# Block sums of the normed tokens formed by TensorE in PSUM, with the x rows loaded first, in a decoder layer on one core

## The chip, the core and the metric

The program runs on one core of a Trainium2 chip. TensorE (PE) multiplies matrices and writes to PSUM, eight banks of 128 partitions x 512 f32 words; VectorE (DVE), ScalarE (ACT) and GpSimd (POOL) work on elements; SyncE (SP), ACT and POOL issue DMA transfers between the chip's memory and the core's SBUF. Each engine works through its own instructions in order and waits on semaphores of the others. The metric is the device time of one execution in microseconds (us), lower is better. All times here are of this one core.

## What is computed

One decoder layer on 512 tokens of width 1024: a SwiGLU feed-forward block (FFN 1), a mixer (RWKV-7 heads beside differential attention), and a second feed-forward block (FFN 2), each with an RMS norm before and after:

```python
for l in range(DEPTH):
    h = rmsnorm(x, ffn1_pre_g[l])
    x = x + FFN_RES * rmsnorm(swiglu(h, ffn1_w_gate[l], ffn1_w_up[l], ffn1_w_down[l]), ffn1_post_g[l])
    h = rmsnorm(x, mix_pre_g[l])
    ...
    x = x + rmsnorm(y, mix_post_g[l])
    h = rmsnorm(x, ffn2_pre_g[l])
    x = x + FFN_RES * rmsnorm(swiglu(h, ffn2_w_gate[l], ffn2_w_up[l], ffn2_w_down[l]), ffn2_post_g[l])
```

with `rmsnorm(x, g) = x * rsqrt(mean(x * x) + eps) * g` per token and `swiglu(h) = (silu(h @ w_gate) * (h @ w_up)) @ w_down`.

## The kernel before

**Precision.** The large products run on rounded operands (F32R). To keep f32 accuracy each operand is split into a rounded part and a remainder (`parts`: ACT rounds, DVE subtracts), and a product is three matmuls: high by high, high by low, low by high (L615, L617, L618 in the FFN).

**Strassen-Winograd blocks.** The gate and up products of an FFN (class `FFN`) take the 1024 input features in two halves and the 512 tokens in two halves. Seven products replace eight, numbered 1 to 7, for each of 11 pairs of weight tiles. Their token operands are `B11` and `B21` (the first 256 tokens, lower and upper features), `B22` (last 256 tokens, upper features) and four block sums, T1 = B12 - B11, T2 = B22 - T1, T3 = B22 - B12, T4 = B21 - T2. Each operand is stored as features on partitions, tokens along the row, split in two parts. The weight operands are sums as well (`g_weights`, on DVE) and are split by `wparts`.

**Slots.** `g_slots` lists 77 (pair, product) slots; a slot (`g_product`) is 24 matmuls of 128x128 by 256 columns. The first four need only B11 and B21; the fifth, (0, 5), needs T1. `stream` prepares the weights of a slot AHEAD = 2 slots before its products; they sit in three rotating pairs of tiles.

**Where the token operands come from.** `start` (FFN 1) loads the four token tiles of 128 rows, takes the norm's factor (`rms`, ACT squares and DVE reciprocal) and scales on ACT (L511). For FFN 2 `norms` does the same behind the output projection (tail key "o") and scales on DVE (L311). Then `feat` handles the tile: eight transposes of 128x128 f32 into two PSUM banks that take turns (L527), a multiplication by the gain on DVE from PSUM to an f32 buffer (`h32`, L530), and for tiles 0 and 1 the split into B11 and B21 (L494 on ACT, L495 on DVE). For tiles 2 and 3 DVE also forms T1, T2, T3 and T4 from `h32` (L538), and T1, T2, B22, T3 and T4 are split.

**What sets the order.** `Streams` interleaves generators by due times written into the code, and a scheduler then places the instructions of each engine; the resulting order is fixed in the program. The DMA queue of SP takes x tiles, weights and results in program order; the ACT queue takes the rows of gains.

Of the kernel before, what the change touches and what calls it, by code (L numbers as in the profile page):

```python
# [19 lines left out]
P = 128  # L20
T = 512
# [36 lines left out]
def layout(inputs):  # L58
# [38 lines left out]
    rows += [g["mix_pre_g"]]  # L97
# [4 lines left out]
    for p in range(NPR):  # L102
# [21 lines left out]
        "gnb": (3584, 512), "lam": (4096, 256), "gm": (4352, 1024)}  # L124


class Layer:
# [4 lines left out]
    def setup(self, st):  # L132
# [11 lines left out]
        nc.scalar.dma_start(out=self.ident, in_=A["ident"])  # L144
        self.zero = c.tile([P, 1], F32, name="zero")
# [132 lines left out]
    def norms(self, S, br, t, key, ys, half, xsrc, dst, h=None, tb=None, feat=None):  # L278
# [8 lines left out]
        xo, tmp, z = br["xo"][t], br["tmp"], br["z"][t % 2]  # L287
# [22 lines left out]
        if feat is not None:  # L310
            nc.vector.tensor_scalar(out=z, in0=xo, scalar1=r, scalar2=None, op0=ALU.mult)  # L311
            yield 0.0, 0.8
            yield from feat(t, z, tb)
            S.mark(f"{key}z{t}")
            S.mark(f"{key}h{t}", 1.2)
            return
# [57 lines left out]
    def run(self):  # L374
        tc, nc, A = self.tc, self.nc, self.A
        S = self.S = Streams()
        with ExitStack() as st:
# [34 lines left out]
            br = self.bridge(f2.big("F1"), fp, "pgm")  # L412
# [32 lines left out]
class FFN:  # L445
# [37 lines left out]
    def inputs(self):  # L483
        self.B = {n: self.hslot(n) for n in ("B11", "T1", "T2", "B21", "T3", "B22", "T4")}
        self.h32 = self.big("F2")[:, 0:4096].rearrange("p (b k t) -> p b k t", b=4, k=4)
        self.cb = self.bridge_tile()
        self.gst = ExitStack()
        self.gp = self.gst.enter_context(self.tc.tile_pool(name=f"gp{self.i}", bufs=1, reuse_waits="tile"))
        self.raw = {}
# [8 lines left out]
    def start(self, t, src):  # L498

        L, nc, S = self.L, self.nc, self.S  # L500
        if t == 0:
            self.x0 = self.big("F1")
        x = self.x0[:, t * D:(t + 1) * D]
        junk = self.x0[:, 4 * D:5 * D]
        nc.sync.dma_start(out=x, in_=src[t * P:(t + 1) * P, :])
        if t == 1:
            self.load(0, 0)
        yield 0.0, 2.0
        r = L.rms(x, junk, "p")
        yield 0.0, 2.5  # L510
        nc.scalar.activation(x, x, AF.Copy, scale=r)  # L511
# [4 lines left out]
    def feat(self, t, xn, tb):  # L516
# [4 lines left out]
        o, _ = FV[f"g{self.i}"]  # L521
        dst = lambda n: [self.B[n][:, i, :, cs] for i in range(2)]
        for q in range(2):
            pt = L.bank(tb, "pt")
            for j in range(4):
                k = q * 4 + j
                nc.tensor.transpose(pt[:, j * P:(j + 1) * P], xn[:, k * P:(k + 1) * P], L.ident)  # L527
            hv = self.h32[:, q * 2 + half, :, cs]
            g = L.fv[:, o + q * 4:o + q * 4 + 4].unsqueeze(2).to_broadcast([P, 4, P])
            nc.vector.tensor_tensor(out=hv, in0=pt.rearrange("p (k t) -> p k t", k=4), in1=g, op=ALU.mult)  # L530
            if half == 0:
                self.parts(hv, dst(("B11", "B21")[q]))
            yield 0.42, 0.3 if q == 0 else 0.0
        if half == 0:
            return
        B11, B12, B21, B22 = (self.h32[:, i, :, cs] for i in range(4))
        t1, t2, t3, t4 = (self.cb[:, i:i + 512].rearrange("p (k t) -> p k t", k=4) for i in (1024, 1536, 3072, 3584))
        sub = lambda o, a, b: nc.vector.tensor_tensor(out=o, in0=a, in1=b, op=ALU.subtract)  # L538
        sub(t1, B12, B11)
        self.parts(t1, dst("T1"))  # L540
        sub(t2, B22, t1)
        self.parts(t2, dst("T2"))
        self.parts(B22, dst("B22"))
        sub(t3, B22, B12)
        self.parts(t3, dst("T3"))
        sub(t4, B21, t2)
        self.parts(t4, dst("T4"))
        S.mark(f"{self.i}T{t}", 2.0)
# [100 lines left out]
    def stream(self):  # L649
# [8 lines left out]
        for i in range(self.AHEAD):  # L658
# [3 lines left out]
        for i, (m, p) in enumerate(slots):  # L662
# [4 lines left out]
            ahead(i + self.AHEAD)  # L667
            self.g_product(m, p, ws.pop(i))
            self.g_out(m, p)
            yield 2.87, 0.0  # L670
# [724 lines left out]
```

## Time and profile before

| | us |
|---|---|
| median of 3 runs | 1110.42 |
| lowest and highest of these runs | 1110.08, 1114.44 |
| the profiled execution | 1110.48 |
| its span, first to last instruction | 1108.7 |
| PE busy in the span | 1052.6 |
| DVE busy | 726.0 |
| ACT busy | 525.8 |
| POOL busy | 54.5 |

The profile shows one execution. Busy time of an engine counts its operations; the granted clock is TensorE's, as a share of full speed (1.00 is 2.4 GHz, 0.50 is 1.2 GHz). Matmuls are pipelined: a record of 0.28 us can be followed by the next after 0.12 us. A row of a group of instructions gives line, engine, operation, result and sources, shapes and count. FFN 1's products run from 20 to about 253 us, the mixer and the output projection to 737, FFN 2 from there to the end. A few matmul records can be missing from a trace.

### The profile page before, as it was taken

The numbers are of one execution on the slowest core, as the hardware profiler recorded it, in microseconds if no ns is written. First come the engines' busy times: TensorE is split into PE (matmuls) and PEld (weight loads), VectorE is DVE, ScalarE is ACT, GpSimd is POOL, SyncE is SP. The second block draws the span as 40 slices with busy tenths as digits, with TensorE's granted clock in tenths as the row PEclk, the third lists the DMA queues.
The fourth block names the chain that finished last, engine by engine and source line by source line (L and its number), as shares of the span: only waits on it lengthen the run. The fifth ranks groups of instructions, "written<-read, shape, count | busy, mean of one in ns | idle before, by whom it ended". The sixth has DMA issues, their size and how long they took to land.

```text
span 1108.7 us, 17430 instructions
## 1 busy us (share of the span) xinstructions
PE 1052.6 (95%) x7104; PEld 923.1 (83%) x7104; DVE 726.0 (65%) x1131; ACT 525.8 (47%) x849; POOL 54.5 (5%) x64
## 2 busy tenths in 40 slices
PE   4799999999999899999999999986999999999997
PEld 4799999998888696777778776776999999988886
DVE  5987888874333453577744797479888888753335
ACT  7555444553222766623453535365554554542223
POOL 0000000000000101222211110000000000000000
PEclk9899999999999899988998999988999999999999
DMA  7133333205333937653773426321424233043332
GB/s 306 40 114 127 103 92 137 77 1 171 95 95 95 247 94 163 144 118 86 174 175 92 91 57 233 101 95 42 149 79 143 85 114 116 1 152 95 95 95 96
DMA packets 52881, 127.11 MB, mean 115 GB/s; under 512 B 21688, under 2 KB 22072, under 8 KB 52800
## 3 DMA queue, kind: packets, MB, share of 16 engines
q1 hardware_dynamic: 45872, 106.18, 29.1%
q0 software_dynamic: 4320, 14.98, 8.2%
q10 hardware_dynamic: 2608, 4.83, 1.3%
q8 instruction: 56, 0.92, 0.3%
q14 instruction: 25, 0.20, 0.1%
HBM read 116.56 MB, written 7.34 MB: 112 GB/s over the span
## 4 chain that ended last, share of the span: by engine, by line
PE 87%; DVE 6%; ACT 3%; DMA 2%; issue 1%; ACTq 0%; POOL 0%; SPq 0%; DVEq 0%; POOLq 0%
PE gu L615 13%; PE gu L617 13%; PE gu L618 13%; PE y L220 8%; PE y L221 8%; PE y L222 8%; PE pj L220 4%; PE pj L221 4%; PE pj L222 4%; PE sc L1327 1%; PE op L1355 1%; DVE br L538 1%; PE s L1055 1%; DMA F<-in_x 1%; DMA raw<-in_gup 1%
## 5 line engine op out<-in xcount | busy, mean ns | idle before, releaser
L615 PE MATMUL gu<-T,w 128*128 128x256 f32 x704 | 199.9, 284 | 8.5 <-ACT T L494 8.5
L617 PE MATMUL gu<-T,w 128*128 128x256 f32 x704 | 200.0, 284 | 0.6 <-DVE T L495 0.6
L618 PE MATMUL gu<-T,w 128*128 128x256 f32 x704 | 198.6, 282 | 0.0
L494 ACT ACTIVATE w<-raw 128x1024 fp32r<-128x1024 f32 x110 | 116.7, 1061 | 127.2 <-issue 76.0
L209 DVE TENSOR_TENSOR wlo<-raw,whi 128x1024 fp32r<-128x1024 f32 x52 | 63.6, 1224 | 150.7 <-ACT whi L208 150.6
L615 PE MATMUL gu<-B,w 128*128 128x256 f32 x528 | 151.7, 287 | 9.4 <-ACT w L494 7.5
L617 PE MATMUL gu<-B,w 128*128 128x256 f32 x528 | 151.1, 286 | 0.9 <-DVE B L495 0.9
L495 DVE TENSOR_TENSOR w<-raw,w 128x1024 fp32r<-128x1024 f32 x110 | 134.5, 1223 | 24.5 <-ACT w L494 24.4
L618 PE MATMUL gu<-B,w 128*128 128x256 f32 x528 | 150.2, 285 | 0.0
L615 PEld LDWEIGHTS gu<-T,w 128*128 128x128 f32 x704 | 133.1, 189 | 8.7 <-ACT T L494 8.7
L220 PE MATMUL y<-whi,a 128*128 128x512 f32 x352 | 138.9, 395 | 0.0
L222 PE MATMUL y<-whi,a 128*128 128x512 f32 x352 | 138.9, 395 | 0.0
L221 PE MATMUL y<-wlo,a 128*128 128x512 f32 x352 | 138.9, 395 | 0.0
L618 PEld LDWEIGHTS gu<-T,w 128*128 128x128 f32 x704 | 134.5, 191 | 0.2 <-DVE w L495 0.2
L617 PEld LDWEIGHTS gu<-T,w 128*128 128x128 f32 x704 | 133.0, 189 | 0.9 <-DVE T L495 0.9
L208 ACT ACTIVATE whi<-raw 128x1024 fp32r<-128x1024 f32 x52 | 55.0, 1059 | 163.3 <-PE y L221 156.9
L615 PEld LDWEIGHTS gu<-B,w 128*128 128x128 f32 x528 | 101.4, 192 | 9.8 <-ACT w L494 7.7
L617 PEld LDWEIGHTS gu<-B,w 128*128 128x128 f32 x528 | 101.4, 192 | 1.2 <-DVE B L495 1.2
L618 PEld LDWEIGHTS gu<-B,w 128*128 128x128 f32 x528 | 101.9, 193 | 0.0
L220 PE MATMUL pj<-hm,whi 128*128 128x512 f32 x184 | 79.9, 434 | 0.0
L222 PEld LDWEIGHTS y<-whi,a 128*128 128x128 f32 x352 | 66.3, 188 | 15.5
L221 PEld LDWEIGHTS y<-wlo,a 128*128 128x128 f32 x352 | 66.3, 188 | 15.4
(293 smaller groups left out, 1844.5 us busy)
## 6 DMA issues: line engine op xcount, KB each, us to landing
raw<-in_wgu SPq DMA_DIRECT2D x88, 512.0 KB, 4.4
raw<-in_wd SPq DMA_DIRECT2D x44, 512.0 KB, 3.6
raw<-in_win SPq DMA_DIRECT2D x27, 512.0 KB, 5.7
wlo<-in_win POOLq DMA_DIRECT2D x24, 512.0 KB, 5.6
raw<-in_wo SPq DMA_DIRECT2D x8, 512.0 KB, 4.3
F<-in_x SPq DMA_DIRECT2D x4, 512.0 KB, 4.8
br<-in_x SPq DMA_DIRECT2D x4, 512.0 KB, 6.3
xd<-br SPq DMA_DIRECT2D x4, 512.0 KB, 5.2
```

The costliest lines, as they stand in the source:

```text
L208: nc.scalar.activation(hi[:, :m], src, AF.Copy)
L209: (eng or nc.vector).tensor_tensor(out=lo[:, :m], in0=src, in1=hi[:, :m], op=ALU.subtract)
L220: mm(ps, lhsT=a[0], rhs=b[0], start=first, stop=False)
L221: mm(ps, lhsT=a[0], rhs=b[1], start=False, stop=False)
L222: mm(ps, lhsT=a[1], rhs=b[0], start=False, stop=last)
L494: nc.scalar.activation(dst[0], src, AF.Copy)
L495: nc.vector.tensor_tensor(out=dst[1], in0=src, in1=dst[0], op=ALU.subtract)
L538: sub = lambda o, a, b: nc.vector.tensor_tensor(out=o, in0=a, in1=b, op=ALU.subtract)
L615: mm(ps[:, j], lhsT=w[0][:, j, ks], rhs=B[:, 0, k], start=p in (1, 2, 5) and j == 0 and k == 0, stop=False, **kw)
L617: mm(ps[:, j], lhsT=w[0][:, j, ks], rhs=B[:, 1, k], start=False, stop=False, **kw)
L618: mm(ps[:, j], lhsT=w[1][:, j, ks], rhs=B[:, 0, k], start=False, stop=last, **kw)
L1055: nc.tensor.matmul(pv[e][:, i, :, :], lhsT=BK[rs, c, :, :], rhs=self.XR[p][rs, c, e:e + 2, :], start=True, stop=True)
```

## The change

The gain is multiplied in before the transposition: FFN 1's scaling moves from ACT to DVE and multiplies by the norm's factor and a gain row at once (`row_g1`, a new transfer to all partitions), FFN 2's scaling does the same in two halves (`row_g2`). `feat` then has TensorE write B11, B21 and B22 as transposes and T1 to T4 as accumulated products: each term of a sum is a plain f32 product of a token tile with the identity or with its negative (`nident`, a new tile), added up in the PSUM bank. A late tile's sums take 2, 3, 2 and 4 terms for four feature groups each: 8 + 12 + 8 + 16 = 44 products and 4 transposes. ACT and DVE split straight from PSUM. The scaled token tiles are kept (FFN 1 in `F1`, FFN 2 in four slices of `F2`), since tiles 2 and 3 read tiles 0 and 1 again. The four x tiles are issued ahead of any weights, and `stream` prepares three slots of weights before the first product and the next one behind a slot's products, no longer ahead of them.

```diff
--- before.py
+++ after.py
@@ -94,7 +94,7 @@
     a["fv"] = fv
     rows = [g["ffn1_post_g"], g["mix_post_g"], g["ffn2_post_g"], g["rwkv_gn_w"], g["rwkv_gn_b"]]
     rows += [g[f"diff_lam_{n}"] for n in ("q1", "k1", "q2", "k2")]
-    rows += [g["mix_pre_g"]]
+    rows += [g["mix_pre_g"], g["ffn1_pre_g"], g["ffn2_pre_g"]]
     a["rows"] = np.ascontiguousarray(np.concatenate(rows)).reshape(1, -1)
     rk = np.zeros((P, NPR, 8), f32)
     ind = np.zeros((P, NPR, 8), f32)
@@ -121,7 +121,7 @@
 
 
 ROWS = {"pg1": (0, 1024), "pgm": (1024, 1024), "pg2": (2048, 1024), "gnw": (3072, 512),
-        "gnb": (3584, 512), "lam": (4096, 256), "gm": (4352, 1024)}
+        "gnb": (3584, 512), "lam": (4096, 256), "gm": (4352, 1024), "g1": (5376, 1024), "g2": (6400, 1024)}
 
 
 class Layer:
@@ -142,6 +142,8 @@
         nc.scalar.dma_start(out=self.fv, in_=A["fv"])
         self.ident = c.tile([P, P], F32, name="ident")
         nc.scalar.dma_start(out=self.ident, in_=A["ident"])
+        self.nident = c.tile([P, P], F32, name="nident")
+        nc.vector.tensor_scalar(out=self.nident, in0=self.ident, scalar1=-1.0, scalar2=None, op0=ALU.mult)
         self.zero = c.tile([P, 1], F32, name="zero")
         nc.vector.memset(self.zero, 0.0)
         self.eps = c.tile([P, 4], F32, name="eps")
@@ -284,7 +286,7 @@
             yield f"{key}z{t - 2}"
         if t not in br["xo"]:
             self.fetch(br, t, xsrc)
-        xo, tmp, z = br["xo"][t], br["tmp"], br["z"][t % 2]
+        xo, tmp, z = br["xo"][t], br["tmp"], br["z"][t % len(br["z"])]
         ss2 = self.sp.tile([P, 2], F32, tag="oss2", name="oss2")
         for i in range(2):
             nc.scalar.activation(tmp[:, hs[i]], ys[i], AF.Square, accum_out=ss2[:, i:i + 1])
@@ -308,7 +310,9 @@
         yield 0.0, 3.0
         nc.sync.dma_start(out=dst[t * P:(t + 1) * P, :], in_=xo)
         if feat is not None:
-            nc.vector.tensor_scalar(out=z, in0=xo, scalar1=r, scalar2=None, op0=ALU.mult)
+            for i in range(2):
+                nc.vector.scalar_tensor_tensor(out=z[:, hs[i]], in0=xo[:, hs[i]], scalar=r, in1=br["g"][:, hs[i]],
+                                               op0=ALU.mult, op1=ALU.mult)
             yield 0.0, 0.8
             yield from feat(t, z, tb)
             S.mark(f"{key}z{t}")
@@ -409,7 +413,9 @@
             fp = st.enter_context(tc.tile_pool(name="f2", bufs=1, reuse_waits="tile"))
             f2 = FFN(self, 2, fp, fp, hp, hx)
             f2.inputs()
-            br = self.bridge(f2.big("F1"), fp, "pgm")
+            br = self.bridge(f2.big("F1"), fp, "pgm", "g2")
+            z4 = f2.big("F2")
+            br["z"] = [z4[:, t * D:(t + 1) * D] for t in range(NT)]
             kts = [4, 5, 6, 7, 0, 1, 2, 3]
             YK = [self.ktile(YT, k) for k in range(KT)]
             ys = [[self.bank(b, "y") for _ in range(2)] for b in ((0, 1), (4, 5), (6, 7), (2, 3))]
@@ -482,7 +488,7 @@
 
     def inputs(self):
         self.B = {n: self.hslot(n) for n in ("B11", "T1", "T2", "B21", "T3", "B22", "T4")}
-        self.h32 = self.big("F2")[:, 0:4096].rearrange("p (b k t) -> p b k t", b=4, k=4)
+        self.xn = {}
         self.cb = self.bridge_tile()
         self.gst = ExitStack()
         self.gp = self.gst.enter_context(self.tc.tile_pool(name=f"gp{self.i}", bufs=1, reuse_waits="tile"))
@@ -500,15 +506,16 @@
         L, nc, S = self.L, self.nc, self.S
         if t == 0:
             self.x0 = self.big("F1")
+            nc.sync.dma_start(out=self.x0[:, 0:D], in_=src[0:P, :])
+            self.grow = L.row(self.bp, "g1", "g")
+            for i in range(1, NT):
+                nc.sync.dma_start(out=self.x0[:, i * D:(i + 1) * D], in_=src[i * P:(i + 1) * P, :])
+            self.junk = self.bp.tile([P, D], F32, tag="pg", name="junk")
         x = self.x0[:, t * D:(t + 1) * D]
-        junk = self.x0[:, 4 * D:5 * D]
-        nc.sync.dma_start(out=x, in_=src[t * P:(t + 1) * P, :])
-        if t == 1:
-            self.load(0, 0)
         yield 0.0, 2.0
-        r = L.rms(x, junk, "p")
+        r = L.rms(x, self.junk, "p")
         yield 0.0, 2.5
-        nc.scalar.activation(x, x, AF.Copy, scale=r)
+        nc.vector.scalar_tensor_tensor(out=x, in0=x, scalar=r, in1=self.grow, op0=ALU.mult, op1=ALU.mult)
         yield 0.0, 0.6
         yield from self.feat(t, x, (0, 1))
         S.mark(f"ph{t}", 1.2)
@@ -518,34 +525,31 @@
         L, nc, S = self.L, self.nc, self.S
         half, c0 = t // 2, (t % 2) * P
         cs = slice(c0, c0 + P)
-        o, _ = FV[f"g{self.i}"]
-        dst = lambda n: [self.B[n][:, i, :, cs] for i in range(2)]
-        for q in range(2):
+        self.xn[t] = xn
+        x2, x0 = xn, self.xn.get(t - 2)
+        B11, B21 = (x2, 0, 1), (x2, 4, 1)
+        if half == 0:
+            todo = [("B11", [B11]), ("B21", [B21])]
+        else:
+            p = lambda x, k: (x, k, 1)
+            n = lambda x, k: (x, k, -1)
+            todo = [("T1", [p(x2, 0), n(x0, 0)]), ("T2", [p(x2, 4), n(x2, 0), p(x0, 0)]), ("B22", [p(x2, 4)]),
+                    ("T3", [p(x2, 4), n(x2, 0)]), ("T4", [p(x0, 4), n(x2, 4), p(x2, 0), n(x0, 0)])]
+        for name, terms in todo:
             pt = L.bank(tb, "pt")
-            for j in range(4):
-                k = q * 4 + j
-                nc.tensor.transpose(pt[:, j * P:(j + 1) * P], xn[:, k * P:(k + 1) * P], L.ident)
-            hv = self.h32[:, q * 2 + half, :, cs]
-            g = L.fv[:, o + q * 4:o + q * 4 + 4].unsqueeze(2).to_broadcast([P, 4, P])
-            nc.vector.tensor_tensor(out=hv, in0=pt.rearrange("p (k t) -> p k t", k=4), in1=g, op=ALU.mult)
-            if half == 0:
-                self.parts(hv, dst(("B11", "B21")[q]))
-            yield 0.42, 0.3 if q == 0 else 0.0
-        if half == 0:
-            return
-        B11, B12, B21, B22 = (self.h32[:, i, :, cs] for i in range(4))
-        t1, t2, t3, t4 = (self.cb[:, i:i + 512].rearrange("p (k t) -> p k t", k=4) for i in (1024, 1536, 3072, 3584))
-        sub = lambda o, a, b: nc.vector.tensor_tensor(out=o, in0=a, in1=b, op=ALU.subtract)
-        sub(t1, B12, B11)
-        self.parts(t1, dst("T1"))
-        sub(t2, B22, t1)
-        self.parts(t2, dst("T2"))
-        self.parts(B22, dst("B22"))
-        sub(t3, B22, B12)
-        self.parts(t3, dst("T3"))
-        sub(t4, B21, t2)
-        self.parts(t4, dst("T4"))
-        S.mark(f"{self.i}T{t}", 2.0)
+            for k in range(4):
+                o = pt[:, k * P:(k + 1) * P]
+                for i, (x, k0, sign) in enumerate(terms):
+                    xk = x[:, (k0 + k) * P:(k0 + k + 1) * P]
+                    if len(terms) == 1:
+                        nc.tensor.transpose(o, xk, L.ident)
+                    else:
+                        nc.tensor.matmul(o, lhsT=xk, rhs=L.ident if sign > 0 else L.nident, start=k == 0 and i == 0,
+                                         stop=k == 3 and i == len(terms) - 1, skip_group_check=True)
+            self.parts(pt.rearrange("p (k t) -> p k t", k=4), [self.B[name][:, i, :, cs] for i in range(2)])
+            yield 0.45 * len(terms), 0.0
+        if half:
+            S.mark(f"{self.i}T{t}", 0.5)
 
 
     def load(self, m, half):
@@ -655,7 +659,7 @@
         def ahead(i):
             if i < len(slots):
                 ws[i] = self.wparts(*slots[i])
-        for i in range(self.AHEAD):
+        for i in range(self.AHEAD + 1):
             ahead(i)
         for t in range(2):
             yield "po"[self.i - 1] + f"h{t}"
@@ -664,9 +668,9 @@
                 yield key + "T2"
                 yield key + "T3"
                 self.F = [self.big(f"F{j}").rearrange("p (k t) -> p k t", t=T) for j in (1, 2)]
-            ahead(i + self.AHEAD)
             self.g_product(m, p, ws.pop(i))
             self.g_out(m, p)
+            ahead(i + self.AHEAD + 1)
             yield 2.87, 0.0
         self.gst.close()
         dst = ExitStack()
```

TensorE's order at the start of FFN 1, before, from its first instruction (`pt` is a PSUM bank for transposes, `gu` one for products):

```order
L527 MATMUL pt_166<-ident_71,F1_110 128x128 x4
L527 MATMUL pt_182<-ident_71,F1_110 128x128 x4
L527 MATMUL pt_174<-ident_71,F1_110 128x128 x4
L527 MATMUL pt_198<-ident_71,F1_110 128x128 x4
L527 MATMUL pt_190<-ident_71,F1_110 128x128 x4
L527 MATMUL pt_210<-ident_71,F1_110 128x128 x4
L615 MATMUL gu_257<-B11_98,w_118 128x256
L617 MATMUL gu_257<-B11_98,w_118 128x256
```

The same place now:

```order
L545 MATMUL pt_177<-ident_71,F1_111 128x128 x4
L545 MATMUL pt_184<-ident_71,F1_111 128x128 x4
L545 MATMUL pt_191<-ident_71,F1_111 128x128 x4
L545 MATMUL pt_198<-ident_71,F1_111 128x128 x4
L619 MATMUL gu_331<-B11_100,w_122 128x256
L619 MATMUL gu_361<-B21_103,w_126 128x256
L547 MATMUL pt_205<-ident_71,F1_111 128x128
L547 MATMUL pt_205<-nident_73,F1_111 128x128
```

The sum groups stand among the products of the first two slots: T1 and T2 of tile 2 (8 and 12 products) come when only two of the 48 products have been issued, the other groups follow at intervals, and slots three and four stand behind all of them. In FFN 2 the first two slots are whole, T1 and T2 of tile 2 come behind them, and the rest stands within slots three and four.

DVE's order at the start of FFN 1, before, from the middle of the gain multiplications (`br` is the buffer of the sums):

```order
L530 TENSOR_TENSOR F2_105<-pt_198,fv_69 128x4x128
L495 TENSOR_TENSOR B11_98<-F2_105,B11_98 128x4x128 x2
L495 TENSOR_TENSOR B21_101<-F2_105,B21_101 128x4x128
L530 TENSOR_TENSOR F2_105<-pt_190,fv_69 128x4x128
L530 TENSOR_TENSOR F2_105<-pt_210,fv_69 128x4x128
L538 TENSOR_TENSOR br_106<-F2_105 128x512
L495 TENSOR_TENSOR B21_101<-F2_105,B21_101 128x4x128
L530 TENSOR_TENSOR F2_105<-pt_204,fv_69 128x4x128
L495 TENSOR_TENSOR T1_99<-br_106,T1_99 128x4x128
L538 TENSOR_TENSOR br_106<-F2_105,br_106 128x512
```

The same place now, from the third of the four scalings:

```order
L518 SCALAR_TENSOR_TENSOR F1_111<-F1_111,pr_162,row_g1_113 128x1024
L231 RECIPROCAL pr_171<-ps_169 128x1
L501 TENSOR_TENSOR B11_100<-pt_177,B11_100 128x4x128
L518 SCALAR_TENSOR_TENSOR F1_111<-F1_111,pr_171,row_g1_113 128x1024
L501 TENSOR_TENSOR B21_103<-pt_184,B21_103 128x4x128
L501 TENSOR_TENSOR w_123<-raw_119,w_122 128x1024
L501 TENSOR_TENSOR B11_100<-pt_191,B11_100 128x4x128
L501 TENSOR_TENSOR w_127<-raw_119,w_126 128x1024
L501 TENSOR_TENSOR B21_103<-pt_198,B21_103 128x4x128
```

The gain multiplications and the sums are gone, the scalings stand ahead, and the weights' remainders have moved up between the blocks' remainders. The third group of transposes (`pt_191`) and the first sum group (`pt_205`) share a bank, so T1 follows the remainder that reads `pt_191`.

## Rows read from the trace of the kernel before

**Rows 1.** Page: busy us, share of the span and instructions of each engine.
```profile
PE 1052.6 (95%) x7104; PEld 923.1 (83%) x7104; DVE 726.0 (65%) x1131; ACT 525.8 (47%) x849; POOL 54.5 (5%) x64
```
**Rows 2.** Stretches, FFN 1's start: us, busy (instructions) per engine, clock, DMA.
```profile
28.00:35.50 7.50, 0.03 (x1) 0.03 (x1) 7.50 (x13) 4.55 (x7) 0.00 (x0) 0.74 0.00 0
```
**Rows 3.** Stretches, FFN 2's start, same columns (PE, PEld, DVE, ACT, POOL, clock).
```profile
742.50:758.50 16.00, 15.90 (x111) 15.66 (x111) 14.56 (x26) 9.84 (x23) 0.00 (x0) 0.81 0.25 99
758.50:766.90 8.40, 0.00 (x0) 0.00 (x0) 8.40 (x13) 3.48 (x7) 0.00 (x0) 0.71 0.00 0
766.90:772.50 5.60, 5.00 (x22) 4.71 (x23) 5.60 (x9) 2.63 (x4) 0.00 (x0) 0.52 0.00 0
780.00:800.00 20.00, 20.00 (x170) 20.00 (x169) 17.57 (x20) 11.30 (x16) 0.00 (x0) 1.00 0.48 157
```
**Rows 4.** Page, costliest groups: busy, mean ns | idle before, by releaser.
```profile
L615 PE MATMUL gu<-T,w 128*128 128x256 f32 x704 | 199.9, 284 | 8.5 <-ACT T L494 8.5
...
L615 PE MATMUL gu<-B,w 128*128 128x256 f32 x528 | 151.7, 287 | 9.4 <-ACT w L494 7.5
```
**Rows 5.** Stretches, line 615 alone: us, PE and PEld busy (records), clock.
```profile
60.00:80.00 20.00, 15.77 (x56) 10.31 (x57) 1.00 0.31 106
```
**Rows 6.** Line 615 on sums (T): ns, first and last start; span, then from 755.
```profile
L615 PE MATMUL gu<-T,w x704: 277/281/582, 42.4 to 978.8; 128*128 128x256 f32 x176
...
L615 PE MATMUL gu<-T,w x60: 277/282/582, 766.9 to 799.7; 128*128 128x256 f32 x60
```
**Rows 7.** Timeline, DVE (start us, length us): weight remainder, gain multiplications, two halves.
```profile
11.32 1.23 DVE L495 TENSOR_TENSOR w<-raw,w 128x1024 fp32r<-128x1024 f32 x1 [0.76 <-ACT w L494]
...
21.09 1.28 DVE L530 TENSOR_TENSOR F<-pt,fv 128x512 f32<-128x512 f32 x2
...
731.27 1.42 DVE L300 SCALAR_TENSOR_TENSOR F<-z,or,F 128x512 f32<-128x512 f32 x2
```
**Rows 8.** Timeline, PE: plain f32 products (L1355) and transposes (L1374) in a row.
```profile
592.61 0.71 PE L1355 MATMUL op<-Vd,pT 128*128 128x128 f32 x4
...
650.50 1.38 PE L1355 MATMUL op<-Vd,pT 128*128 128x128 f32 x10
...
703.04 0.63 PE L1374 MATMUL ot<-ident,on 128*128 128x128 f32 x4
```
**Rows 9.** Timeline, FFN 1's start: gain row issued, first transposes, first warm product.
```profile
1.73 0.39 ACTq L162 DMA_DIRECT2D row_pg<-in_rows  x1
...
8.71 1.11 PE L527 MATMUL pt<-ident,F 128*128 128x128 f32 x4 [8.71 <-ACT F L511]
...
21.42 0.29 PE L617 MATMUL gu<-B,w 128*128 128x256 f32 x1
```
**Rows 10.** PE groups by form, whole span: plain f32 products, transposes.
```profile
L1355 PE MATMUL op<-Vd,pT 128*128 128x128 f32 x80 | 12.6, 288 | 1.2 <-ACT qk L910 1.2
...
L1374 PE MATMUL ot<-ident,on 128*128 128x128 f32 x16 | 2.5, 277 | 0.1
```
**Rows 11.** Chain of work that ended last: start us, length us, what.
```profile
650.56 1.31 PE op L1355 x10
```
**Rows 12.** DMA issues, 0 to 30 us: KB each, median us to landing.
```profile
row_pg<-in_rows ACTq DMA_DIRECT2D x1, 512.0 KB, 7.6
```
**Rows 13.** Timeline, FFN 2's start: scaling on DVE, first product by a weight remainder.
```profile
737.40 0.75 DVE L311 TENSOR_SCALAR z<-F,pr 128x1024 f32<-128x1024 f32 x1
...
742.90 0.41 PE L618 MATMUL gu<-B,w 128*128 128x256 f32 x1
```
**Rows 14.** Stretches within the mixer, PE alone: us, busy (records), clock, DMA.
```profile
585.00:591.00 6.00, 6.00 (x33) 0.50 0.39 112
...
596.00:601.00 5.00, 4.92 (x72) 1.00 0.78 204
610.00:615.00 5.00, 5.00 (x71) 1.00 0.10 21
```
**Rows 15.** Timeline, PE: small f32 products before the clock fell.
```profile
582.22 5.10 PE L1142 MATMUL q<-Q,gm 64*64 64x32 f32 x64
```

## The prediction, made before the changed kernel was run

> **What bounds the kernel now.** I read the page's busy times first: the matmul engine (PE) is busy for 95% of the span and VectorE (DVE) for 65% [rows 1]. A change to DVE's work can only pay where PE stands still, and the two places where it does are the ones the change rewrites. The table of stretches shows both. At the start of FFN 1, from 28.0 to 35.5 us, PE does 0.03 us of work and DVE 7.50 of 7.50; the granted clock falls there, to a mean of 0.74 [rows 2]. Between the mixer and FFN 2, from 758.5 to 766.9, PE does nothing, DVE 8.40 of 8.40, and the clock is 0.71 and then 0.52 [rows 3]. The page's groups say who is waited for: the products that read block sums sat idle 8.5 us for ACT's copy of a sum (T), those that read plain blocks 7.5 us for a weight split queued behind the sums [rows 4]. So the ends of these two stages are set by the chain DVE gain or sum, ACT rounding, DVE remainder, eight times for each of the two late token tiles.
>
> From there on PE is the bound: at 780 to 800 it is busy 20.00 of 20.00 us [rows 3]. L615 is a third of a stage's products and has 56 records in 20 us [rows 5], so a product of 256 columns takes 20/168 = 0.119 us and a slot of 24 takes 2.87. What the change is worth is therefore how much later or earlier the fifth slot begins, the first that needs sums, corrected for half-clock time. In FFN 1 it begins at 42.4 [rows 6], at full clock. In FFN 2 it begins at 766.9, but from there to 772.5 only 22 records were started [rows 3] where 5.6/0.119 = 47 fit; 25 x 0.119 = 3.0 us lost make it equal to 769.9.
>
> **Removed.** Per FFN: eight gain multiplications (L530) and eight sums (L538) on DVE, each 0.69 long; two in a row take 1.28, so each holds DVE for 0.60 [rows 7]. 16 x 0.60 = 9.6 us leave DVE. Of the 16 transposes of the late tiles, 8 stay. A transpose is one record: four take 0.63 with the last one's 0.27 in it, so they follow each other by 0.12 [rows 8]; 8 x 0.12 = 1.0 us leaves PE. In FFN 1 the four scalings by the norm's factor leave ACT.
>
> **Added on PE.** For each late tile 8 + 12 + 8 + 16 = 44 products with the identity or its negative, 88 per FFN. They are plain f32 products, 128x128 by 128 columns. The row of the same shape is L1355: the loop issues it 40 times (four heads, 1 + 2 + 3 + 4) and the trace has 80 records, while L1374, a transpose issued 16 times, has 16 [rows 10]. So a plain f32 product is two records with a weight load each. Ten of them take 1.38 us in the timeline with the last one's 0.27 in it, (1.38 - 0.27)/9 = 0.123; in the chain the same ten take 1.31, which gives 0.115 [rows 8, 11]. I take 0.118, a product at 0.236: **88 x 0.236 = 20.8 us per FFN**. Bounds: 0.115 (20.2 us) and the 0.145 of the shorter run of four in 0.71 (25.5 us) [rows 8].
>
> The Trainium skill would make this dearer: "TensorE: Matmul & The Clock Gate", Terms, calls the transpose mode four times faster for FP32, and "FP8 and Floating Point Precision", TensorE Precision Notes, gives true FP32 four passes. By that a product would cost four transposes; the trace, with two records, has half of it. I go by the trace, and take the rule as a rival below.
>
> **Start of FFN 1.** The scaling by the norm's factor now also multiplies by the gain row, on DVE, so it waits for the row. Its transfer takes the place of row_pg in ACT's queue, issued at 1.73 and landed 7.6 later: 9.3 [rows 9, 12]. The four x tiles now stand at the head of SP's queue, so they are there in time and the row is the later one. The four scalings are not in the trace; two halves of the kind (L300) take 1.42, one 1024-wide sum 1.23 [rows 7, 9]; I take 1.25. DVE's order then holds the four scalings, three remainders of 0.60 and one weight split (1.13 of DVE, its 1.23 less the overlap of two in a row), up to the remainder that frees the bank for the first sum group: 9.3 + 4 x 1.25 + 3 x 0.60 + 1.13 = 17.2, with the small operations between them 17.3. From there the PE queue is 88 products (20.8), 8 transposes (1.0) and the 96 products of the first four slots (96 x 0.119 = 11.5), and nothing in it waits long, because a group of 8 to 16 products (1.9 to 3.8 us) covers the 1.3 us that ACT and DVE need to empty the other bank. A cold start costs more: the first transposes take 1.11 for four instead of 0.63, and records of 0.28 to 0.29, the warm size, are first seen at 21.42 [rows 8, 9], five us after the steady work begins; I charge 2.0 of such five us. Fifth slot at 17.3 + 20.8 + 1.0 + 11.5 + 2.0 = 52.6 instead of 42.3: **+10.3 us**. What DVE gave up hides nothing, since PE is late next.
>
> **Start of FFN 2.** Up to the first products little changes. On DVE two halves (1.32) replace the one scaling (0.75, L311) per tile, four gain multiplications of 0.60 go, and the first product that needs the weights' remainder, at 742.9 before, I put at 743.2 [rows 13]. From 742.5 PE did the four slots and 16 transposes by 758.5, half-clock time included [rows 3]: 16.0 us. After: 743.0 + 16.0 - 1.0 + 20.8 = 778.8 for the fifth slot. The clock should not fall again, as PE no longer stops. Against 769.9: **+8.9 us**.
>
> The remaining edits get nothing. Weights split one slot further ahead stand in the same place among the products, because the call moved past them; the added row of FFN 2 goes out together with the one that was already loaded there, while the output projection still runs; the negative identity is one 128x128 operation while DVE waits for x.
>
> Sum: 10.3 + 8.9 = 19.2 us. The profiled execution took 1110.48 us (span 1108.7), the median of the runs is 1110.42. **1110.5 + 19.2 = 1129.7 us.**
>
> **Rivals.**
> 1. The product costs one record, as a transpose does (the identity might be treated so). Then 88 x 0.118 = 10.4 per FFN: 20.8 us less, 1108.9, not slower. The line between the two: apart from the products the change gives 41.5 - 19.2 = 22.3 us back, so 176 products break even at 0.127 us each. Against it: 80 records for 40 calls [rows 10]. For it: only that the operand is an identity. 8 in 100; a third of that reaches a gain of over 0.5%.
> 2. The clock falls during the products, though PE works. It fell in the middle of unbroken small f32 products (L1142, 32 columns) and stood at 0.50 from 585 to 591; but from 596 to 601 and 610 to 615, attention and recurrence in f32, it stayed at 1.00 [rows 14, 15]. At half clock a product doubles; if half of them run so, 88 x 0.236 = 20.8 more: 1150.5. 7 in 100.
> 3. A product costs four transposes, 0.48 us: 176 x 0.244 = 43 more, 1172.6. No row shows that. This is the rule named above. 2 in 100.
> 4. The sums overlap with less loss than I add up (an earlier row, no cold penalty): FFN 1 at best 15.5 + 20.2 + 1.0 + 11.5 = 48.2, +5.9; FFN 2 +8.0; 1124. This is inside my range.
>
> **How the numbers follow.** The forecast, two records at full clock with PE as the bound, has 80 in 100. The range runs from the low bounds (1124, and two us for a start that I place too late) to the price of 25.5 us per FFN and a first group 1.5 us later, 1129.7 + 9.4 + 1.5 = 1141: **1122 to 1141**. Left outside: rivals 1 to 3 and 3 in 100 that something hides most of the loss. About 0.5%, 5.6 us, is what a measurement of this kernel can tell from no change. Slower by more: 0.80 + 0.07 + 0.02 + 0.02 = 0.91; within: 0.06; faster by more: 0.03.
>
> **What the profile after would show.** L547 with 352 records for 176 products, 0.115 to 0.123 us apart; PE without a hole between 17 and 53 us and between 743 and 779; the first product on a sum at 52 to 53 and near 779 instead of 42.4 and 766.9 [rows 6]; DVE with idle time in both stretches, waiting for PE or for ACT's copy of a bank; the granted clock at 1.00 from about 749 on. Wrong would be: 176 records; a clock of 0.50 inside the products; or PE waiting for the bank that DVE has to free.

## The result, and the profile after

The changed kernel takes 1128.79 us (median of four runs, 1124.45 to 1131.30) beside 1111.41 of the kernel before: the ratio is 1.0158, 95% interval 1.0128 to 1.0188, or 17 us slower (14 to 21). The forecast was 1129.7. The profiled execution took 1126.74 us, its span is 1124.9, 16.2 longer than before.

The page's first part, busy time, share of the span and instructions of each engine, answers to [rows 1]; the last two lines are its groups of products, busy and mean ns, then the idle time just before them, and answer to [rows 4]:

```profile
PE 1084.8 (96%) x7440; PEld 956.8 (85%) x7440; DVE 715.9 (64%) x1108; ACT 521.2 (46%) x845; POOL 54.7 (5%) x64
...
L619 PE MATMUL gu<-T,w 128*128 128x256 f32 x704 | 198.7, 282 | 0.0
...
L619 PE MATMUL gu<-B,w 128*128 128x256 f32 x528 | 151.2, 286 | 0.5 <-ACT B L500 0.5
```

DVE has 10 us less to do and PE 32 us more; PE's 336 more records are 352 of the products less 16 transposes. The waits of 8.5 and 7.5 us in front of the first products [rows 4] are gone. What stands in their place shows in the table of stretches (length, then busy time and records of PE, PEld, DVE, ACT and POOL, granted clock, DMA), which answers to [rows 2, 3]:

```profile
28.00:35.50 7.50, 7.50 (x70) 7.50 (x69) 1.58 (x3) 1.36 (x3) 0.00 (x0) 1.00 0.01 2
42.30:53.00 10.70, 10.70 (x93) 10.70 (x92) 6.35 (x7) 3.32 (x4) 0.00 (x0) 1.00 0.01 2
742.50:751.00 8.50, 5.08 (x25) 3.41 (x23) 7.53 (x16) 7.23 (x21) 0.00 (x0) 0.96 0.40 161
751.00:758.00 7.00, 6.38 (x33) 6.38 (x34) 6.96 (x12) 4.04 (x7) 0.00 (x0) 0.56 0.20 76
758.00:786.30 28.30, 28.30 (x249) 28.02 (x248) 16.98 (x23) 10.14 (x19) 0.00 (x0) 1.00 0.05 20
```

The hole of FFN 1 is closed: from 28.0 to 35.5 PE works all 7.50 us and DVE 1.58 of them, where it was 0.03 and 7.50 before. The hole of FFN 2 is closed too, 28.30 of 28.30 us up to 786.3. PE fills them with the products that form the sums, and then runs on for longer than the holes had been. The first product that reads a sum starts later in both FFNs (line 619 on T: ns, first and last start; answers to [rows 6], 42.4 and 766.9):

```profile
L619 PE MATMUL gu<-T,w x16: 281/283/285, 53.0 to 58.4; 128*128 128x256 f32 x16
...
L619 PE MATMUL gu<-T,w x31: 278/281/285, 786.3 to 799.9; 128*128 128x256 f32 x31
```

FFN 1 is 10.6 us late. In FFN 2, against the 769.9 that stands for 766.9 without the half-clock time behind it, it is 16.4, which is also what the end of the span lost. At first sight FFN 2 thus adds 5.8 us to FFN 1's. But the last product of the output projection starts only 8.5 us after its counterpart (timeline of PE, before and in the changed kernel; the third line is FFN 2's first product that needs a remainder of weights, here at 751.62 and at 742.9 before):

```profile
736.70 0.40 PE L222 MATMUL y<-whi,yt 128*128 128x512 f32 x1
...
745.19 0.40 PE L224 MATMUL y<-whi,yt 128*128 128x512 f32 x1
...
751.62 0.58 PE L622 MATMUL gu<-B,w 128*128 128x256 f32 x1 [1.65 <-DVE w L501]
```

So about 2 us of FFN 1's loss had come back in between, and FFN 2 itself adds 7.9. They came back in the mixer, where PE's clock fell at other places. Two stretches of before:

```profile
412.00:424.00 12.00, 11.22 (x47) 8.41 (x47) 7.53 (x9) 11.24 (x18) 1.72 (x2) 0.86 0.53 99
510.00:536.00 26.00, 22.88 (x121) 18.09 (x120) 17.72 (x40) 7.84 (x12) 7.99 (x9) 0.87 0.51 121
```

and their counterparts in the changed kernel. The first is as long as before, but at a clock of 1.00 in place of 0.86, and it holds 53 records of PE in place of 47; the second holds the same 121 records in 1.3 us less:

```profile
422.40:434.40 12.00, 10.96 (x53) 7.94 (x52) 7.53 (x9) 11.51 (x18) 1.72 (x2) 1.00 0.47 93
519.80:544.50 24.70, 21.57 (x121) 16.83 (x121) 17.74 (x40) 7.85 (x12) 8.01 (x9) 0.93 0.58 134
```

PE's 2019 products of the mixer are the same in both traces and stand in the same order, so I don't count this to the change. Executions of one kernel differ by as much: the profiled execution of the changed kernel is 2 us below its median.

The products themselves are line 547 (ns, first and last start):

```profile
L547 PE MATMUL pt<-ident,F x192: 270/275/421, 19.0 to 784.1; 128*128 128x128 f32 x192
L547 PE MATMUL pt<-nident,F x160: 275/275/421, 19.5 to 784.4; 128*128 128x128 f32 x160
...
  ACT T L500: 33.2, 16
```

192 + 160 = 352 records for 176 products: two each. The last line says who waited for them: ACT, 16 times, 33.2 us in all. Before, PE waited for ACT and DVE; now ACT, which rounds the sums, waits for PE. Their pace shows in the timeline of PE (start, length), a pair of records in each row:

```profile
27.99 0.38 PE L547 MATMUL pt<-ident,F 128*128 128x128 f32 x2
28.21 0.39 PE L547 MATMUL pt<-nident,F 128*128 128x128 f32 x2
28.43 0.39 PE L547 MATMUL pt<-ident,F 128*128 128x128 f32 x2
28.66 0.39 PE L547 MATMUL pt<-nident,F 128*128 128x128 f32 x2
28.88 0.39 PE L547 MATMUL pt<-ident,F 128*128 128x128 f32 x2
```

From 27.99 to 28.88 there are four products, 0.222 us each, 0.111 per record.

### The profile page after: what moved, and what is told of

Read it like the earlier page. It is cut to its first block, busy times and chain, and to the rows that moved or that the text cites. A ratio compares the mean times of both kernels' runs of the same rounds, so it can differ in the third digit from the quotient of the medians.

```text
span 1124.9 us, 18081 instructions
## 1 busy us (share of the span) xinstructions
PE 1084.8 (96%) x7440; PEld 956.8 (85%) x7440; DVE 715.9 (64%) x1108; ACT 521.2 (46%) x845; POOL 54.7 (5%) x64
## 4 chain that ended last, share of the span: by engine, by line
PE 89%; DVE 4%; ACT 3%; DMA 2%; issue 1%; ACTq 0%; POOL 0%; DVEq 0%; POOLq 0%
PE gu L619 13%; PE gu L622 13%; PE gu L621 13%; PE y L222 8%; PE y L223 8%; PE y L224 8%; PE pj L222 4%; PE pt L547 4%; PE pj L223 4%; PE pj L224 3%; PE sc L1331 1%; PE op L1359 1%; PE s L1059 1%; DMA row_g<-in_rows 1%; DMA raw<-in_gup 1%
## 5 line engine op out<-in xcount | busy, mean ns | idle before, releaser
L224 PEld LDWEIGHTS y<-whi,a 128*128 128x128 f32 x352 | 66.3, 188 | 15.6
L222 PEld LDWEIGHTS y<-whi,a 128*128 128x128 f32 x352 | 66.3, 188 | 15.3
```

The source lines that it names most:

```text
L222: mm(ps, lhsT=a[0], rhs=b[0], start=first, stop=False)
L224: mm(ps, lhsT=a[1], rhs=b[0], start=False, stop=last)
```

## Experiments

**Theory:** the loss is the PE time of the products, at two records each, less what DVE gave up; nothing else in the change moves the end by more than 2 us. **Rivals:** a product has another price (one record, or four transposes); or the loss comes from the gain row, the two banks or the reordered loads, and the products are hidden. The medians of before that the ratios below go by were 1110.85, 1111.35 and 1110.43.

### More products: pair

```diff
-            todo = [("T1", [p(x2, 0), n(x0, 0)]), ("T2", [p(x2, 4), n(x2, 0), p(x0, 0)]), ("B22", [p(x2, 4)]),
-                    ("T3", [p(x2, 4), n(x2, 0)]), ("T4", [p(x0, 4), n(x2, 4), p(x2, 0), n(x0, 0)])]
+            todo = [("T1", [p(x2, 0), n(x2, 0), p(x2, 0), n(x0, 0)]),
+                    ("T2", [p(x2, 0), n(x2, 0), p(x2, 4), n(x2, 0), p(x0, 0)]), ("B22", [p(x2, 4)]),
+                    ("T3", [p(x2, 4), n(x2, 4), p(x2, 4), n(x2, 0)]),
+                    ("T4", [p(x0, 4), n(x0, 4), p(x0, 4), n(x2, 4), p(x2, 0), n(x0, 0)])]
```

> The changed kernel with a zero-sum pair of products added to every block of the four sums: each block first adds a row block and takes it away again. 64 more products per FFN, 128 in all, nothing else changed. My theory (PE is the bound there, a product is two records and costs 0.222 us warm): 128 x 0.222 = 28.4 us more than the changed kernel, 1157 us, a little more if the early ones run at the low clock. If a product cost one record of 0.12 (rival 1): +15. If it cost four transposes, 0.48 (rival 3): +61. If the loss of the change came from something other than the products (the wait for the gain row, the bank): about 0, 1129.

Measured: 1158.34 us, ratio to before 1.0433 (1.0397 to 1.0469), 29.5 more than the changed kernel: 29.5/128 = 0.231 us per product. The first product on a sum in FFN 1, line 621 here, moved from 53.0 to 67.0:

```profile
L621 PE MATMUL gu<-T,w x68: 278/280/283, 67.0 to 99.8; 128*128 128x256 f32 x68
```

14.0 us for 64 products are 0.219 each. This is the price of two records; 15 us (one record) and 61 us (four transposes) are both out of reach, and so is "hidden".

### Fewer products: first_mm and first_tr

Both leave terms out, so that the sums aren't formed; the first replaces them by one product for each block, the second by one transpose.

```diff
+            todo = [("T1", [p(x2, 0)]), ("T2", [p(x2, 4)]), ("B22", [p(x2, 4)]), ("T3", [p(x2, 4)]), ("T4", [p(x0, 4)])]
...
-                    if len(terms) == 1:
+                    if name[0] == "B":
```

The second hunk is in first_mm alone.

> Each block of the four sums is made of its first term alone, as one product with the identity (the other terms are left out, so the sums are not formed): 32 products per FFN in place of 88. If products are the loss and PE stays the bound: 112 x 0.222 = 24.9 us less than the changed kernel, 1104. But a group is now 4 products, 0.9 us, shorter than the 1.3 us that ACT and DVE need to empty a bank, so PE may wait for the other bank: 1104 to 1110. If products cost nothing on the path: 1129.

> As the kernel with first terms alone, but that term by a transpose in place of a product (the other terms are left out, so the sums are not formed): 32 transposes where that one has 32 products per FFN. If a product costs 0.10 us more than a transpose and PE is the bound: 6.5 us less than it, 1098. If PE waits for the two banks to be emptied, the same time as with products, 1104 to 1110: then the emptying is next behind the products.

Measured: 1104.94 us (ratio 0.9948, 0.9925 to 0.9971) and 1097.87 (0.9897, 0.9867 to 0.9927). 112 products fewer gave 23.9 us, 0.213 each. 64 transposes in place of 64 products gave another 7.1, 0.110 each, where 0.222 - 0.12 = 0.10 was due. The two banks, which I had feared, cost little: PE is busy without a gap from 20 to 53 us in either, and stands for 0.6 to 0.7 us at FFN 2's start. With the sums for nothing the kernel would thus be faster than before by 13 us (by the medians) or 11 (by the ratio, 8 to 15).

### The sums elsewhere: sums_dve and sums_pool

The sums are formed from the scaled token tiles ahead of the transposing, four subtractions of 512 columns for a late tile, on DVE or on GpSimd (`nc.gpsimd` in the line with `nc.vector`), and then transposed.

```diff
+            lo, hi = slice(0, 512), slice(512, 1024)
+            t1, t2, t3, t4 = (self.cb[:, i:i + 512] for i in (1024, 1536, 3072, 3584))
+            for o, a, b in ((t1, x2[:, lo], x0[:, lo]), (t2, x2[:, hi], t1), (t3, x2[:, hi], x2[:, lo]),
+                            (t4, x0[:, hi], t2)):
+                nc.vector.tensor_tensor(out=o, in0=a, in1=b, op=ALU.subtract)
+            todo = [("T1", [(t1, 0, 1)]), ("T2", [(t2, 0, 1)]), ("B22", [(x2, 4, 1)]), ("T3", [(t3, 0, 1)]),
+                    ("T4", [(t4, 0, 1)])]
```

> The changed kernel with the four sums formed on DVE from the scaled rows, before the transposing (four subtractions of 512 columns per late tile), and 20 transposes per late tile in place of 44 products and 4 transposes. PE loses 15.7 us of work per FFN, DVE gains 8 x 0.60 = 4.8. If PE stayed the bound: 1129 - 31 = 1098; with part of DVE's 4.8 us per FFN and of the waits for the two banks on the path: 1103, range 1097 to 1110, below the kernel before (1111), since the gain multiplications of DVE stay away. Rival: DVE's chain binds again as it did before the change: 1111 or more.

> As the kernel with the sums formed on DVE from the scaled rows (1109), with the eight subtractions per FFN on GpSimd (POOL), which has nothing to do in either stretch. POOL's own subtractions and products of this shape take 1.0 to 1.5 us in the trace against 0.6 to 0.7 on DVE. If DVE's chain is what holds that kernel (its trace has holes of PE at 35 to 42 and 760 to 770 and DVE full), taking 4.8 us per FFN off it gives 5 to 10 us: 1099 to 1104, near the 1098 of the kernel that leaves the sums out. If POOL's slower operations become the wait, or the two engines slow each other down at the SBUF: 1109 or more.

On DVE: 1109.13 us, ratio 0.9976 (0.9945 to 1.0008), no difference from before that can be measured, at the upper end of what I expected. Its table of stretches says why (columns as above):

```profile
35.50:42.30 6.80, 5.00 (x36) 4.18 (x34) 6.80 (x8) 3.20 (x4) 0.00 (x0) 1.00 0.00 1
755.00:770.00 15.00, 9.72 (x59) 8.62 (x59) 14.37 (x21) 5.21 (x8) 0.00 (x0) 0.80 0.00 0
```

DVE is full and PE has holes again; the waits of PE from 755 to 775 us (in total, times, longest) name the subtractions, line 538:

```profile
PE pt L548 <- DVE br L538: 3.8, 2, 3.2
```

So the eight subtractions, 4.8 us of DVE per FFN, cost 1109.13 - 1097.87 = 11.3 us for both FFNs against the kernel that leaves the sums out. That is the mechanism of the rival "DVE's chain binds again", and I had given it too little. On GpSimd: 1097.29 us, ratio 0.9892 (0.9835 to 0.9950), a little below the 1099 to 1104 that I expected. It can't be told from the time of the kernel without sums, and it is faster than both the kernel before and the changed one. The stretch that was worst on DVE:

```profile
745.00:760.00 15.00, 11.46 (x90) 10.17 (x89) 14.88 (x19) 6.88 (x13) 7.65 (x5) 1.00 0.03 11
```

DVE is still full, but the clock stays at 1.00. The first product on a sum starts at 753.8, which is 25.2 us behind the last product of the output projection; with the sums on DVE it was 27.1, with half-clock time to follow.

### The change in one FFN alone: prod_f1 and prod_f2

The FFN that is left out has the norm's scaling, `feat` and the order of the weights of the kernel before, and FFN 1 its loads of x. Of prod_f1 (prod_f2 has `OLD = (1,)`):

```diff
+    OLD = (2,)
...
+        if self.i in self.OLD:
+            yield from self.feat_old(t, xn, tb)
+            return
```

> The change in FFN 1 alone; FFN 2 as before the change. My theory: the first use of a sum moves from 42.4 to 53.0 in FFN 1 (+10.6, of which 1.9 came back in the profiled execution by half-clock stretches of the mixer that fell otherwise): 1111 + 8.5 to 10.6 = 1119.5 to 1121.5. Rival: the loss is nearly all in FFN 2, where the first sum was used 19 us later: 1112.

> The change in FFN 2 alone; FFN 1 as before the change. My theory: +7.9 us, 1119. If the two halves do not add up (for instance because the loss in FFN 2 depends on when FFN 1 ends): far from 17.4 less what the kernel with FFN 1 alone shows.

Measured: 1119.31 us with the change in FFN 1 alone (ratio 1.0082, 1.0056 to 1.0109) and 1119.36 in FFN 2 alone (1.0060, 1.0032 to 1.0088). By the ratios that is 9.1 and 6.7 us (by the medians 8.0 each), 15.8 in all, beside 17.6 for both. The halves add up within their intervals, and neither FFN is alone to blame.

### The edits costed at nothing: rows_ahead and sums_pool_late

rows_ahead is the kernel before with the x rows loaded first, the weights one slot further ahead and the negative identity. sums_pool_late is the kernel with the sums on GpSimd and the weights where they were before the change; these lines of it differ from sums_pool:

```diff
-        for i in range(self.AHEAD + 1):
+        for i in range(self.AHEAD):
...
+            ahead(i + self.AHEAD)
             self.g_product(m, p, ws.pop(i))
             self.g_out(m, p)
-            ahead(i + self.AHEAD + 1)
```

> Both FFNs with transposes, gain multiplications and sums on DVE as before the change, but with what I costed at nothing kept: all four loads of x at the head of the queue, the weights split one slot further ahead, the negative identity. My theory: 1111, within 2 us. If these edits hide a gain or a loss of their own: more than 3 us off, and the price of the products in the sum is then wrong by as much.

> The kernel with the sums on GpSimd (1097), with the weights split at the place where they were before the change, one slot later than the change has them. DVE is full from 20 to 42 us there, and one weight combination and its split stand in front of the remainders of the sums. If the place of the split costs nothing, as I assumed: 1096 to 1099. If DVE's order matters: the first use of a sum moves by up to 2.4 us per FFN, 1092 to 1102.

Measured: 1113.73 us, ratio 1.0022 (0.9995 to 1.0050), and 1099.92, ratio 0.9883 (0.9833 to 0.9933). The first can't be told from before and leaves room for a loss of 5 us at most; its median is 2.4 above before's, a little more than the 2 us that I allowed. Its trace shows where such a loss would be. In FFN 1 the first product on a sum starts at 41.0, 1.4 earlier than before, but the last product of FFN 1 starts at 375.4 in both. In FFN 2 the first product on a sum starts at 765.2, but the output projection ends 4.0 earlier here (732.7), so this is 2.3 later than before, counted from there. The second can't be told from sums_pool: its first product on a sum starts at 37.7 in FFN 1, as there.

### The gain row earlier: after_row and sums_pool_row

```diff
-            self.grow = L.row(self.bp, "g1", "g")
+            o, n = ROWS["g1"]
+            self.grow = self.bp.tile([P, n], F32, tag="g", name="row_g1", bufs=1)
+            nc.sync.dma_start(out=self.grow, in_=L.A["rows"][:, o:o + n].to_broadcast([P, n]))
```

> The changed kernel with the gain row of FFN 1 loaded on the queue of x right behind the first tile. My sum put the start of the first group of products at the row's landing plus 8 us of DVE. If that is so: first scaling at about 7.5 and first product at 16.8 to 17.5 (19.05 before), first use of a sum 1 to 2 us before 53.0. If the start is set by the statistics of the x tiles on ACT or by the low clock: 52.5 to 53.5.

> The kernel with the sums on GpSimd (1097), with the gain row of FFN 1 loaded on the queue of x right behind the first tile, and not on ACT's queue behind the constants. DVE waited 2.4 us for that row before its first scaling at 9.43. If the row starts the chain: first scaling at 7.2 to 8.0 and the fifth slot up to 1.5 us earlier, 1096; the later x tiles come 1.3 us later and may take it back: then 1097 to 1098.

In the changed kernel, one execution of 1123.86 us. The first scaling starts at 7.85, not 9.76, and the first products come at 15.86, not 19.05 and earlier than the 16.8 to 17.5 expected (timeline of PE, with the products before and behind the place where the pace changes):

```profile
15.86 0.80 PE L549 MATMUL pt<-ident,F 128*128 128x128 f32 x2 [0.72 <-DVE B L501]
...
18.16 0.64 PE L549 MATMUL pt<-nident,F 128*128 128x128 f32 x2
18.58 0.58 PE L549 MATMUL pt<-ident,F 128*128 128x128 f32 x2
19.00 0.39 PE L549 MATMUL pt<-nident,F 128*128 128x128 f32 x2
19.22 0.39 PE L549 MATMUL pt<-ident,F 128*128 128x128 f32 x2
```

The first product on a sum starts at 49.8, 3.2 earlier and more than the 1 to 2 expected. The row moved the first scaling by 1.9, but DVE's order changed as well. With the later x tiles behind the row, the fourth scaling (19.10) and the first two weight splits (16.76, 17.98) came to stand behind the remainders that free the banks (15.12), and the first sums need tiles 0 and 2 alone; tile 2 itself is scaled later than before (13.85, not 13.07). How much of the 3.2 us belongs to the row alone this run doesn't separate. With the sums on GpSimd the same edit gives nothing: 1099.99 us (ratio 0.9900, 0.9856 to 0.9943) and a first product on a sum at 38.1, not 37.7, although the first scaling is at 7.76 and not 9.43. There tile 2 is scaled later all the same (at 13.77, not 12.73), GpSimd's first subtraction follows it at 15.13, not 14.10, and PE waits 2.3 us for a sum of GpSimd up to 19.90, so the gain is gone before the main products start.

### The same runs, stage by stage

The times above carry the mixer's own spread. The traces allow a reading without it: FFN 1 up to the start of its last product, then up to the start of the last product of the output projection, then FFN 2 up to the end of the span (us, one execution each).

| kernel | FFN 1 | mixer and projection | FFN 2 |
|---|---|---|---|
| before | 375.4 | 361.3 | 372.0 |
| the change | 385.7 | 359.5 | 379.7 |
| prod_f1 | 385.5 | 360.1 | 372.0 |
| prod_f2 | 376.4 | 355.6 | 379.7 |
| pair | 399.7 | 367.6 | 393.0 |
| first_mm | 373.1 | 362.4 | 367.6 |
| first_tr | 368.5 | 361.7 | 364.6 |
| sums_dve | 374.9 | 362.4 | 370.9 |
| sums_pool | 370.4 | 358.2 | 367.9 |
| sums_pool_late | 370.4 | 366.8 | 368.6 |
| sums_pool_row | 371.4 | 362.2 | 367.9 |
| rows_ahead | 375.4 | 357.3 | 374.5 |
| after_row | 382.5 | 361.0 | 378.6 |

The mixer lasts from 355.6 to 367.6 us, though no run touches its code. Where two kernels have the same code in an FFN, that FFN agrees within 0.3 us in four pairs of six and differs by 1.0 and 1.2 in the other two. The change costs 10.4 us in FFN 1 and 7.7 in FFN 2, and each half alone costs about as much (10.1 and 7.7). The zero-sum products of pair cost 14.0 + 13.2 us, 0.213 each; the 112 products that first_mm leaves out, 12.6 + 12.1 us, 0.22 each. Against first_tr, which forms no sums, the sums cost 17.2 + 15.1 us on TensorE, 6.4 + 6.3 on DVE and 1.9 + 3.3 on GpSimd. The 5 us on GpSimd don't show in the times of the runs; in the profiled execution of sums_pool the mixer was 3.5 us shorter than in that of first_tr. rows_ahead loses nothing in FFN 1 and 2.4 us in FFN 2, where it differs from before only in the weights one slot further ahead.

## Why the prediction was right, step by step

**The bound and its place held.** The loss sits where the sum put it: prod_f1 and prod_f2 give 9.1 and 6.7 us where +10.3 and +8.9 stood, and the trace gives 10.6 and 7.9. PE has no hole in either place any more, and DVE idles there, as the prediction said it would.

**The price of a product was the term to get right, and two records were right.** The records of line 1355 [rows 10] told it, against the transposes that do the same job in one. The size was a little off: 0.111 us per record, below my low bound of 0.115. The products thus cost 88 x 0.222 = 19.5 us per FFN, not 20.8. The rows it came from were a short run and a chain, and ten records are too few to read a pace to 5%.

**The start of FFN 1 was too early, and made up for it.** The list of DVE's work up to the first group of products was right, instruction by instruction, but 17.3 became 19.05. The timeline of DVE:

```profile
9.76 1.28 DVE L518 SCALAR_TENSOR_TENSOR F<-F,pr,row_g 128x1024 f32<-128x1024 f32 x1 [2.54 <-DMA row_g<-in_rows]
...
11.68 1.28 DVE L518 SCALAR_TENSOR_TENSOR F<-F,pr,row_g 128x1024 f32<-128x1024 f32 x1
...
14.93 1.28 DVE L518 SCALAR_TENSOR_TENSOR F<-F,pr,row_g 128x1024 f32<-128x1024 f32 x1
16.12 0.69 DVE L501 TENSOR_TENSOR B<-pt,B 128x512 fp32r<-128x512 f32 x1
16.72 1.22 DVE L501 TENSOR_TENSOR w<-raw,w 128x1024 fp32r<-128x1024 f32 x1
17.86 0.69 DVE L501 TENSOR_TENSOR B<-pt,B 128x512 fp32r<-128x512 f32 x1
```

The row came 0.5 later than assumed, the second scaling began 0.6 behind the end of the first (0.3 of it a wait for ACT's root), and the small operations between them did the rest up to 18.55, where the last remainder ends; the first product of a sum is issued 0.5 after it. From there to the fifth slot it took 53.0 - 19.05 = 33.95 us: 19.5 for products, 12.5 for slots and transposes, and 1.95 are left for a cold start that I had put at 2.0; nine products at 0.43 us in place of 0.222 account for 1.8 of it. That the row holds up the first scaling is shown by after_row. So 1.3 us too many for the products stand against 1.75 too few for the start, and 52.6 against 53.0 looks better than it is: two errors that happen to cancel. (The sum also took 42.3 for the 42.4 of [rows 6], and 743.0 where the sentence before has 743.2; neither matters here.)

**FFN 2** has the same error in the products: 751.62 (the first product that needs a remainder of weights) to 786.3 is 34.7 us, where 743.2 to 778.8 is 35.6. The clock was foreseen at 1.00 from 749 on, that is 757.5 with the 8.5 us of shift; the stretches above have 0.56 up to 758 and 1.00 from there.

**Not foreseen** were the 1.9 us that came back in the mixer. They lie within what one execution differs from the next, and the forecast can't claim them. Nor is the total to be taken too exactly: 18.1 us by the stages and 17.4 by the medians stand against the 19.2 of the forecast.

**The rivals.** One record for each product: out, by 352 records and by pair. A clock that falls in the products: their pace was 0.43 us for the first nine, from 19.05 to 22.88, which is the slow start and no fall, and 0.222 from then on; those of FFN 2 all lie in a stretch at 1.00. Four transposes for a product: out, since first_tr gained 0.110 us for each product replaced and not 0.36; a product here costs 0.222/0.12, near two transposes. Four was the Trainium skill's rule ("TensorE: Matmul & The Clock Gate", Terms; "FP8 and Floating Point Precision", TensorE Precision Notes), and the trace doesn't bear it out. The rest of the change, put at 22.3 us without products, comes out of first_tr near that: 13.0 us below before by the medians with 64 transposes in their place, 64 x 0.12 = 7.7, together 20.7.

**What stays open:** whether the earlier weights, costed at nothing, cost anything in the changed kernel. In the order of the kernel before, FFN 2 is 2.4 us longer with them (rows_ahead, one trace); with the sums on GpSimd it is 0.7 shorter with them (sums_pool against sums_pool_late). No run takes them back in the changed kernel itself.

## What to carry to other kernels

Work taken from a waiting engine pays only if its new place has room: here PE was idle for 8 us in each FFN and was given 20. Look for the engine that is idle in that very stretch; GpSimd, slower for each operation than DVE, made the same sums for some 5 us where DVE took 13 and TensorE 32 (by the stages, against no sums), and the time was 1097 us in place of 1129. Count records in the trace, not calls in the code, before a plain f32 product takes the place of a transpose.

## What the runs showed of the hardware

**DVE and GpSimd slow each other, but only in some operations.** Timeline of DVE with the sums on GpSimd:

```profile
18.59 0.68 DVE L501 TENSOR_TENSOR B<-pt,B 128x512 fp32r<-128x512 f32 x1
19.19 1.69 DVE L501 TENSOR_TENSOR w<-raw,w 128x1024 fp32r<-128x1024 f32 x1
...
23.03 2.30 DVE L501 TENSOR_TENSOR w<-raw,w 128x1024 fp32r<-128x1024 f32 x1
25.26 1.27 DVE L501 TENSOR_TENSOR T<-pt,T 128x512 fp32r<-128x512 f32 x2
26.46 1.21 DVE L501 TENSOR_TENSOR w<-raw,w 128x1024 fp32r<-128x1024 f32 x1
```

and of GpSimd (POOL) in the same kernel:

```profile
21.99 2.26 POOL L538 TENSOR_TENSOR br<-F 128x512 f32<-128x512 f32 x1
24.33 2.17 POOL L538 TENSOR_TENSOR br<-F,br 128x512 f32<-128x512 f32 x1
27.62 1.30 POOL L538 TENSOR_TENSOR br<-F 128x512 f32<-128x512 f32 x1 [1.12 <-PE pt L548]
```

A weight remainder, whose two inputs lie in SBUF, takes 1.21 us alone and 1.69 to 2.30 beside a subtraction of GpSimd, which itself takes 2.26 in place of 1.30. A remainder with one input in PSUM keeps its 0.68. The Trainium skill ("SBUF — State Buffer", SBUF: two separate sides) says that a DVE operation with two SBUF inputs and a GpSimd operation that reads SBUF share a pair of ports, one at a time. Which operations suffer here agrees with that.

**The clock.** It stayed at 1.00 through FFN 2's identity products (759.64 to 784.4, with main products between them), and through the stretch of 745 to 760 us in which PE worked 11.46 of 15.00 us. At the start the pace of 0.43 us per product, about half of the later one, ended at 22.9 us in the changed kernel and at 18.6 with the earlier gain row. PE's first transposes start at 11.10 and 9.19 in these two, so the earlier start went with the earlier full pace. The table of stretches gives a granted clock of 1.00 from 8 to 22.9 us all the same: that the slow pace is the lower of the two levels is inferred from the pace and not shown by this column.
